# Gate/up weight sums of a tuned decoder trunk: two by DVE and two by accumulating DMA, and five whole pairs instead of six

## The chip, the core and the metric

The kernel runs on one core of a Trainium2 chip. The metric is the device time of one execution in microseconds, the median of several runs. Engines are called PE (TensorE matmul), PEld (its weight load), DVE (VectorE), ACT (ScalarE), POOL (GpSimd) and SP (SyncE, which here only issues DMAs).

## What is computed

A decoder trunk of two layers on 512 tokens of width 1024, all in float32. Each layer is half a SwiGLU feed-forward block, a mixer (MLA and GLA heads in layer 0, NSA in layer 1) and another half SwiGLU block; a final norm ends it. The change touches the four feed-forward blocks alone:

```python
def swiglu(x, w_gate, w_up, w_down):
    return (jax.nn.silu(x @ w_gate) * (x @ w_up)) @ w_down

for layer in range(DEPTH):           # DEPTH = 2, D_MODEL = 1024, D_FF = 2816, SEQ = 512
    h = h + 0.5 * swiglu(rms_norm(h, ffn_norm[layer, 0]), ...)
    ...                              # the mixer of this layer
    h = h + 0.5 * swiglu(rms_norm(h, ffn_norm[layer, 1]), ...)
```

## The kernel before

Activations lie as eight tiles of 128 channels x 512 tokens. Every float32 factor is split in two float32r parts, a high and a low one (`split`, L149: ACT casts to the high part at L150, DVE subtracts at L151 to get the low part), and every product is three matmuls (`mm3`, L143: L145 high x high, L146 with the low part of the activations, L147 with the low part of the weights).

A feed-forward block (`ffn_body`, L353) walks over 22 column blocks j of 128 hidden columns. A column block needs a gate weight g and an up weight u, each 128 x 1024 (eight chunks of 128 input channels side by side). There are two ways to do a block:

- **A whole pair** (`whole`, L367), for j below `NP` = 6: g and u are loaded, split, and multiplied with all eight chunks of the input, 2 x 8 x 3 matmuls of 512 columns. The result is scaled by `rb` (the norm's factor) afterwards, so whole pairs can start before the norm is known.
- **Seven products** (`gate_up` L117 for the weights, `gate_up_steps` L311 for the matmuls), for j from `NP` on. A Strassen-Winograd form of the 2 x 2 block product [g0 g1; u0 u1] x [x11 x12; x21 x22], where g0, g1 are the halves of g over input channels 0-511 and 512-1023, and the x parts are the input halves by channel and token: seven products of 4 x 3 matmuls of 256 columns. It wants four sums of weight halves (the two halves of tiles `sa` and `sb`, made by DVE at L130 to L133 from the raw loads of g and u) and seven forms of the input (`ffn_forms` L272, tiles `bh`/`bl`, which DVE makes at L283 to L300 and splits). The forms need `rb`, and four of the seven are split only when the last whole pair has let go of its input tiles (`xh`/`xl`), because they share 14 buffers.

The down projection is cut in units of 128 output channels (`unit`, L391): one load of 4 or 5 x 128 columns of w_down, its split, 12 or 15 matmuls into `ps_d`, and one DVE addition to the residual (L398). The units of one group of column blocks are spread over the blocks of the next.

All weight loads go by SP, in one queue, into three buffers `raw` of 512 KB; the split parts have three buffers `whi`/`wlo` (g and down weights) and three `shi`/`slo` (sums), and one `uhi`/`ulo`. The order on each engine is set by a scheduler from a modelled timeline; each engine then runs its list strictly in order and waits at semaphores. POOL does nothing in these stages.

## Time and profile before

| | before |
|---|---|
| median of 3 runs | 2013.54 us (2011.16 to 2014.27) |
| the profiled execution | 2011.51 us, of which the span of the core is 2009.7 us |
| PE, share of the span | 98% |
| DVE | 74% |
| ACT | 51% |
| POOL | 11% |
| mean granted TensorE clock | 0.994 |
| DMA traffic | 186.42 MB, mean 93 GB/s |

Busy shares are means over stages. The four feed-forward blocks lie at about 4 to 366, 596 to 950, 950 to 1304 and 1636 to 2008 us of the span; the mixers stand after the first and after the third. Time in the profile is counted from the first instruction; a matmul's row shows its way through the array, so rows overlap, and the pace is read from start to start.

### The profile page before, as it was taken

What the parts mean: (1) busy time and instruction counts of PE and PEld (TensorE: products, weight loads), DVE (VectorE), ACT (ScalarE), POOL (GpSimd) and SP (SyncE); (2) the same over time, 40 slices, a digit from 0 to 9 for tenths busy, and PEclk for the clock granted to TensorE, in tenths of its full rate; (3) what the DMA queues carried; (4) which work ended last, traced back from release to release, by engine and by line L of the source; (5) the groups of instructions that cost most, each with busy time, mean ns of one, the idle gap of its engine ahead of it and who ended that gap; (6) DMA issues with size and microseconds to landing.
All of it is one profiled execution on the core that took longest, in us unless ns stands there. A gap on an engine that the chain in (4) does not pass through costs nothing.

```text
span 2009.7 us, 31399 instructions
## 1 busy us (share of the span) xinstructions
PE 1969.0 (98%) x11986; PEld 1739.2 (87%) x11986; DVE 1491.5 (74%) x2557; ACT 1019.9 (51%) x1849; POOL 214.0 (11%) x255
## 2 busy tenths in 40 slices
PE   8999999999999999999999999999899999999998
PEld 6899998888778899998789999888687878999997
DVE  7877775678878777766877677667899868777774
ACT  6444443575764444444444444445598754444443
POOL 0000000201330000001000000111365410000001
PEclk9999999999999999999999999999899999999999
DMA  5333332321323233322323232344400033233332
GB/s 175 95 95 99 113 96 68 120 64 50 89 77 102 84 102 106 104 95 84 121 90 101 90 114 96 89 147 136 116 1 1 27 120 92 89 103 96 102 95 69
DMA packets 70553, 186.42 MB, mean 93 GB/s; under 512 B 9473, under 2 KB 12289, under 8 KB 70401
## 3 DMA queue, kind: packets, MB, share of 16 engines
q1 hardware_dynamic: 68944, 181.26, 29.2%
q10 hardware_dynamic: 1072, 2.10, 0.3%
q8 instruction: 94, 1.54, 0.3%
q0 software_dynamic: 384, 1.05, 0.2%
q14 instruction: 59, 0.48, 0.1%
HBM read 172.84 MB, written 2.10 MB: 87 GB/s over the span
## 4 chain that ended last, share of the span: by engine, by line
PE 88%; DVE 6%; ACT 2%; issue 2%; DMA 1%; POOL 0%; SPq 0%; ACTq 0%; POOLq 0%; DVEq 0%
PE ps_d L145 8%; PE ps_d L147 8%; PE ps_d L146 8%; PE ps_a L145 6%; PE ps_a L147 6%; PE ps_a L146 6%; PE ps_b L145 5%; PE ps_b L147 5%; PE ps_b L146 5%; PE ps_gu L147 4%; PE ps_gu L146 4%; PE ps_gu L145 4%; PE ps_p L145 3%; PE ps_p L146 3%; PE ps_p L147 3%
## 5 line engine op out<-in xcount | busy, mean ns | idle before, releaser
L150 ACT CAST whi<-raw 128x512 fp32r<-128x512 f32 (+3 forms) x317 | 257.7, 815 | 337.3 <-PE ps_d L146 124.7
L151 DVE TENSOR_TENSOR wlo<-raw,whi 128x512 fp32r<-128x512 f32 (+3 forms) x317 | 303.0, 957 | 80.6 <-ACT whi L150 79.1
L147 PE MATMUL ps_d<-hid,wlo 128*128 128x512 f32 x672 | 265.2, 396 | 0.0
L146 PE MATMUL ps_d<-hid,whi 128*128 128x512 f32 x672 | 264.9, 395 | 0.0
L145 PE MATMUL ps_d<-hid,whi 128*128 128x512 f32 x672 | 263.6, 395 | 0.0
L145 PE MATMUL ps_a<-bh,shi 128*128 128x256 f32 x768 | 216.9, 282 | 0.0
L146 PE MATMUL ps_a<-bl,shi 128*128 128x256 f32 x768 | 216.4, 282 | 0.0
L147 PE MATMUL ps_a<-bh,slo 128*128 128x256 f32 x768 | 216.2, 281 | 0.0
L216 POOL TENSOR_TENSOR ssq<-ssq,sq 128x512 f32<-128x512 f32 x30 | 46.1, 1538 | 1098.5 <-ACT sq L215 1098.5
L147 PEld LDWEIGHTS ps_d<-hid,wlo 128*128 128x128 f32 x672 | 126.1, 188 | 29.1 <-DVE wlo L151 0.7
L145 PEld LDWEIGHTS ps_d<-hid,whi 128*128 128x128 f32 x672 | 126.1, 188 | 27.1 <-ACT whi L150 1.0
L146 PEld LDWEIGHTS ps_d<-hid,whi 128*128 128x128 f32 x672 | 126.2, 188 | 25.2
L146 PEld LDWEIGHTS ps_a<-bl,shi 128*128 128x128 f32 x768 | 144.7, 188 | 1.2
L145 PEld LDWEIGHTS ps_a<-bh,shi 128*128 128x128 f32 x768 | 144.1, 188 | 1.2
L147 PEld LDWEIGHTS ps_a<-bh,slo 128*128 128x128 f32 x768 | 145.0, 189 | 0.0
L130 DVE TENSOR_TENSOR sa<-raw 128x512 f32<-128x512 f32 x64 | 44.2, 690 | 128.6 <-DMA raw<-wgu 128.6
L398 DVE SCALAR_TENSOR_TENSOR x<-ps_d,x 128x512 f32<-128x512 f32 x152 | 104.0, 686 | 44.3 <-PE ps_d L147 44.0
L612 POOL TENSOR_TENSOR pr<-pr,sums 128x128 f32<-128x128 f32 (+3 forms) x160 | 115.0, 748 | 101.1 <-DVE sums L1034 29.0
L150 ACT CAST uhi<-raw 128x512 fp32r<-128x512 f32 x64 | 39.7, 621 | 162.5 <-PE ps_b L146 104.0
L150 ACT CAST shi<-sa 128x1024 fp32r<-128x1024 f32 x64 | 67.3, 1051 | 80.1 <-PE ps_a L146 76.6
L151 DVE TENSOR_TENSOR slo<-sa,shi 128x1024 fp32r<-128x1024 f32 x64 | 78.3, 1223 | 29.3 <-ACT shi L150 27.3
L593 ACT ACTIVATE pr<-sm_s,sm_m 128x512 f32<-128x512 f32 (+3 forms) x160 | 89.7, 563 | 16.8 <-DVE sm_m L589 15.8
(452 smaller groups left out, 5583.2 us busy)
## 6 DMA issues: line engine op xcount, KB each, us to landing
raw<-wgu SPq DMA_DIRECT2D x175, 512.0 KB, 3.8
raw<-wd SPq DMA_DIRECT2D x96, 256.0 KB, 2.7
raw<-wd SPq DMA_DIRECT2D x64, 320.0 KB, 2.9
raw<-wo SPq DMA_DIRECT2D x32, 256.0 KB, 2.8
raw<-w1t SPq DMA_DIRECT2D x16, 512.0 KB, 3.8
raw<-w0v SPq DMA_DIRECT2D x8, 512.0 KB, 3.7
raw<-w0t SPq DMA_DIRECT2D x6, 512.0 KB, 3.7
rt_s<-rt_f SPq DMA_DIRECT2D x48, 64.0 KB, 2.0
```

What stands on the lines that cost most here:

```text
L130: V.tensor_add(av[:, :w], g[:, :w], u[:, :w])
L145: mm(ps, lh, rh, start=start, stop=False, **k)
L146: mm(ps, lh, rl, start=False, stop=False, **k)
L147: mm(ps, ll, rh, start=False, stop=stop, **k)
L150: self.nc.scalar.copy(hi, src)
L151: self.nc.vector.tensor_sub(lo, src, f32v(hi))
L216: (nc.vector if last or fast else nc.gpsimd).tensor_add(acc, acc, sq)
L398: V.scalar_tensor_tensor(out=self.x[c], in0=ps, scalar=0.5, in1=self.x[c], op0=ALU.mult, op1=ALU.add)
L593: nc.scalar.activation(p, s[:, :n], AF.Exp, bias=mn, scale=-1.0, accum_out=sums)
L612: self.nc.gpsimd.tensor_mul(o, o, w[:, qb : qb + 1].to_broadcast([P, n]))
```

## The change

- `NP` falls from 6 to 5: in each feed-forward block one column block goes from a whole pair to seven products (four in all; 68 blocks by seven products instead of 64). The generator that makes the input forms is run to its end before the first seven products, so that its six steps fit in five whole pairs.
- `gate_up` no longer loads u to a `raw` buffer. A new `load_sums`, traced two column blocks ahead, loads u to `sa` (512 KB) and the first half of u to `sb` (256 KB) by SP, behind the last weight load traced so far. Then two DMAs of 256 KB issued from POOL add in flight: g0 to `sb`'s first half, u1 to `sa`'s first half. DVE makes the other two sums (L141 and L142 of the changed kernel), the last of them into a new tile `sc`.
- `sa` and `sb` have two buffers each instead of one; the third pair of split parts (`uhi`/`ulo`) now holds `sc`. The sums are the same four up to sign and place, and the products take them in another order.

```diff
--- before.py
+++ after.py
@@ -27,7 +27,7 @@
 NEG = -1e30
 TINY = 1e-30
 GROUPS = ((0, 4), (4, 9), (9, 14), (14, 18), (18, 22))
-NP = 6
+NP = 5
 WARM = 11
 H = T // 2
 AHEAD = 400
@@ -88,7 +88,7 @@
         t = self.wp.tile([P, 1024], F32, name="raw", tag="raw", bufs=3)
         for i in range(parts):
             c = slice(i * n // parts, (i + 1) * n // parts)
-            self.nc.sync.dma_start(out=t[:, c], in_=src[:, c])
+            self.load = self.nc.sync.dma_start(out=t[:, c], in_=src[:, c])
         return t
 
     def wparts(self):
@@ -96,9 +96,6 @@
 
     def sparts(self):
         return (self.fw.tile([P, 1024], R, name=n, tag=n, bufs=3) for n in ("shi", "slo"))
-
-    def sum_tile(self, tag):
-        return self.fw.tile([P, 1024], F32, name=tag, tag=tag, bufs=1)
 
     def open_sums(self):
 
@@ -114,30 +111,41 @@
             self.split(raw[:, c], hi[:, c], lo[:, c])
         return hi, lo
 
+    def load_sums(self, f, j):
+
+        nc = self.nc
+        g, u = self.a["wgu"][f, j, 0], self.a["wgu"][f, j, 1]
+        h0, h1 = slice(0, T), slice(T, 2 * T)
+        av, bv = (self.fw.tile([P, 1024], F32, name=n, tag=n, bufs=2) for n in ("sa", "sb"))
+        with self.tc.issue_after(self.load.ins):
+            nc.sync.dma_start(out=bv[:, h0], in_=u[:, h0])
+            nc.sync.dma_start(out=av, in_=u)
+        nc.gpsimd.dma_start(out=bv[:, h0], in_=g[:, h0], accum_op=ALU.add)
+        nc.gpsimd.dma_start(out=av[:, h0], in_=u[:, h1], accum_op=ALU.add)
+        self.sums[j] = av, bv
+
     def gate_up(self, f, j):
 
 
         V, a = self.nc.vector, self.a
         w = T
+        h0, h1 = slice(0, w), slice(w, 2 * w)
+        av, bv = self.sums.pop(j)
+        cv = self.fw.tile([P, w], F32, name="sc", tag="sc", bufs=1)
         g = self.raw(a["wgu"][f, j, 0], 1024)
         gh, gl = self.wparts()
         self.split(g, gh, gl)
-        u = self.raw(a["wgu"][f, j, 1], 1024)
         ah, al = self.sparts()
         bh, bl = self.sparts()
-        uh, ul = (self.fw.tile([P, w], R, name=n, tag=n, bufs=1) for n in ("uhi", "ulo"))
-        av, bv = (self.sum_tile(n) for n in ("sa", "sb"))
-        V.tensor_add(av[:, :w], g[:, :w], u[:, :w])
-        V.tensor_add(av[:, w:], u[:, :w], u[:, w:])
-        V.tensor_add(bv[:, :w], av[:, w:], g[:, :w])
-        V.tensor_add(bv[:, w:], bv[:, :w], g[:, w:])
+        ch, cl = (self.fw.tile([P, w], R, name=n, tag=n, bufs=1) for n in ("uhi", "ulo"))
+        V.tensor_add(bv[:, h1], av[:, h0], g[:, h0])
+        V.tensor_add(cv, bv[:, h1], g[:, h1])
+        self.split(bv, bh, bl)
         self.split(av, ah, al)
-        self.split(bv, bh, bl)
-        self.split(u[:, w:], uh, ul)
-        h0, h1 = slice(0, w), slice(w, 2 * w)
+        self.split(cv, ch, cl)
         return [
-            (gh[:, h0], gl[:, h0]), (gh[:, h1], gl[:, h1]), (ah[:, h0], al[:, h0]), (bh[:, h0], bl[:, h0]),
-            (uh, ul), (ah[:, h1], al[:, h1]), (bh[:, h1], bl[:, h1]),
+            (gh[:, h0], gl[:, h0]), (gh[:, h1], gl[:, h1]), (bh[:, h0], bl[:, h0]), (bh[:, h1], bl[:, h1]),
+            (ah[:, h1], al[:, h1]), (ah[:, h0], al[:, h0]), (ch, cl),
         ]
 
     def mm3(self, ps, lh, ll, rh, rl, start, stop, **k):
@@ -358,6 +366,7 @@
         xs, end = self.ffn_input(gi)
         self.rb = None
         hid, todo, w, forms = {}, [], {}, []
+        self.sums = {}
 
         def done(j, gt, ut):
             V.tensor_mul(ut, gt, ut)
@@ -410,12 +419,16 @@
             g = next(i for i, (j0, j1) in enumerate(GROUPS) if j0 <= j < j1)
             if j == GROUPS[g][0] and g > 0:
                 todo += [(GROUPS[g - 1], c) for c in range(KC)]
+            if NP <= j + 2 < JC:
+                self.load_sums(f, j + 2)
             if NP <= j + 1 < JC:
                 w[j + 1] = self.gate_up(f, j + 1)
             if j < NP:
                 whole(j)
                 next(making, None)
                 if j == NP - 1:
+                    for _ in making:
+                        pass
                     cur = steps(NP)
                     next(cur)
             else:
```

The scheduler's order changes with it in the feed-forward blocks; in the mixers DVE and ACT keep theirs. Three places, all in the first block. A number in a name tells buffers and uses apart; `raw` is a weight load, `wgu` the gate/up and `wd` the down weights.

SP, in the middle of the seven-product blocks, before:

```order
L91 DMA raw_1581<-wd 128x640
L91 DMA raw_1604<-wd 128x640
L91 DMA raw_1627<-wgu 128x1024
L91 DMA raw_1633<-wgu 128x1024
L91 DMA raw_1756<-wd 128x640
L91 DMA raw_1779<-wd 128x640
L91 DMA raw_1802<-wgu 128x1024
L91 DMA raw_1808<-wgu 128x1024
```

and now:

```order
L91 DMA raw_1652<-wd 128x640
L121 DMA sb_1523<-wgu 128x512
L91 DMA raw_1675<-wd 128x640
L122 DMA sa_1522<-wgu 128x1024
L91 DMA raw_1705<-wgu 128x1024
L121 DMA sb_1699<-wgu 128x512
L91 DMA raw_1828<-wd 128x640
L91 DMA raw_1851<-wd 128x640
L122 DMA sa_1698<-wgu 128x1024
```

Between any two g loads there stood one u load and two down loads; now there stand a half and a whole u load for the sums, each in front of a weight load, with the accumulating DMAs on POOL's list.

DVE, blocks 8 to 10, before (L130 to L133 make the sums, L151 splits, L344 and L347 read products, L398 adds a down unit):

```order
L130 TENSOR_TENSOR sa_1291<-raw_1277,raw_1283 128x512
L131 TENSOR_TENSOR sa_1291<-raw_1283 128x512
L151 TENSOR_TENSOR hid_1105<-ut_908,hid_1105 128x512
L344 SCALAR_TENSOR_TENSOR ut_1077<-ps_b_1075,sx_1208 128x256
L151 TENSOR_TENSOR ulo_1141<-raw_1134,uhi_1140 128x512
L347 SCALAR_TENSOR_TENSOR ut_1077<-ps_a_1074,sw_1192 128x256
L151 TENSOR_TENSOR slo_1139<-sb_1143,shi_1138 128x1024
L398 SCALAR_TENSOR_TENSOR x_77<-ps_d_1263,x_77 128x512
L132 TENSOR_TENSOR sb_1292<-sa_1291,raw_1277 128x512
L133 TENSOR_TENSOR sb_1292<-sb_1292,raw_1277 128x512
```

and now (L159 splits, L352 and L355 read products, L407 adds a down unit, L141 makes a sum):

```order
L159 TENSOR_TENSOR slo_1060<-sa_876,shi_1059 128x1024
L407 SCALAR_TENSOR_TENSOR x_77<-ps_d_1182,x_77 128x512
L159 TENSOR_TENSOR wlo_1329<-raw_1326,whi_1328 128x512
L352 SCALAR_TENSOR_TENSOR ut_975<-ps_b_973,sx_1127 128x256
L355 SCALAR_TENSOR_TENSOR ut_975<-ps_a_972,sw_1111 128x256
L141 TENSOR_TENSOR sb_1197<-sa_1196,raw_1353 128x512
L159 TENSOR_TENSOR slo_1212<-sb_1047,shi_1211 128x1024
```

The first row frees the buffer into which `sa_1196` is loaded and accumulated; its reader stands five rows on, ahead of the split of the block before.

DVE where the last whole pair ends and the last four forms (`bl`) are split, before:

```order
L130 TENSOR_TENSOR sa_824<-raw_810,raw_816 128x512
L131 TENSOR_TENSOR sa_824<-raw_816 128x512
L151 TENSOR_TENSOR bl_739<-xf_269,bh_738 128x1024
L132 TENSOR_TENSOR sb_825<-sa_824,raw_810 128x512
L151 TENSOR_TENSOR slo_819<-sa_824,shi_818 128x1024
L133 TENSOR_TENSOR sb_825<-sb_825,raw_810 128x512
L151 TENSOR_TENSOR bl_743<-xf_267,bh_742 128x1024
L386 TENSOR_TENSOR gt_729<-ps_gu_673,rb_254 128x512
L151 TENSOR_TENSOR bl_747<-xf_266,bh_746 128x1024
L151 TENSOR_TENSOR wlo_793<-raw_790,whi_792 128x512
L151 TENSOR_TENSOR bl_751<-xf_268,bh_750 128x1024
L363 TENSOR_TENSOR ut_730<-gt_729,ut_730 128x512
```

and now:

```order
L159 TENSOR_TENSOR bl_635<-xf_269,bh_634 128x1024
L542 SCALAR_TENSOR_TENSOR rope_ang_519<-rope_k_520,rope_ang_519 128x512
L159 TENSOR_TENSOR bl_639<-xf_267,bh_638 128x1024
L542 SCALAR_TENSOR_TENSOR rope_ang_519<-rope_k_520,rope_ang_519 128x512
L159 TENSOR_TENSOR bl_643<-xf_266,bh_642 128x1024
L395 TENSOR_TENSOR ut_623<-ps_gu_597,rb_254 128x512
L159 TENSOR_TENSOR bl_647<-xf_268,bh_646 128x1024
L542 SCALAR_TENSOR_TENSOR rope_ang_519<-rope_k_520,rope_ang_519 128x512
L159 TENSOR_TENSOR slo_722<-sb_534,shi_721 128x1024
L407 SCALAR_TENSOR_TENSOR x_77<-ps_d_672,x_77 128x512
L372 TENSOR_TENSOR ut_623<-gt_622,ut_623 128x512
L159 TENSOR_TENSOR wlo_716<-raw_713,whi_715 128x1024
```

Before, four sums of the second seven-product block stood among the forms; now the split of that block's ready sum, `slo_722`, and the last of the rotary table's steps (`rope`) stand there.

## Rows read from the trace of the kernel before

**Rows 1.** The page: busy us of each engine, share of the span, instructions.
```profile
PE 1969.0 (98%) x11986; PEld 1739.2 (87%) x11986; DVE 1491.5 (74%) x2557; ACT 1019.9 (51%) x1849; POOL 214.0 (11%) x255
```

**Rows 2.** Groups by line and shape: busy us, mean ns | idle before.
```profile
L147 PE MATMUL ps_d<-hid,wlo 128*128 128x512 f32 x672 | 265.2, 396 | 0.0
...
L145 PE MATMUL ps_a<-bh,shi 128*128 128x256 f32 x768 | 216.9, 282 | 0.0
...
L145 PE MATMUL ps_gu<-xh,whi 128*128 128x512 f32 x192 | 76.4, 398 | 4.6 <-DVE gt L386 1.9 <-ACT whi L150 1.3 <-DVE x L580 0.9
```

**Rows 3.** PE's instructions in time, a whole pair: start us, duration us.
```profile
59.90 0.39 PE L145 MATMUL ps_gu<-xh,whi 128*128 128x512 f32 x1
...
69.70 0.39 PE L145 MATMUL ps_d<-hid,whi 128*128 128x512 f32 x1
```

**Rows 4.** The same, products of 256 columns.
```profile
200.03 0.28 PE L145 MATMUL ps_a<-bh,shi 128*128 128x256 f32 x1
...
205.43 0.28 PE L147 MATMUL ps_a<-bh,wlo 128*128 128x256 f32 x1
```

**Rows 5.** Busy time by stretch: first block's forms, other blocks' forms, seven-product stretch.
```profile
core 0: us, PE busy (x) PEld busy (x) DVE busy (x) ACT busy (x) POOL busy (x), PEclk, DMA share, GB/s
34.00:60.00 26.00, 24.09 (x104) 19.36 (x104) 25.78 (x42) 12.09 (x17) 0.00 (x0) 1.00 0.22 72
60.00:75.00 15.00, 15.00 (x66) 12.08 (x65) 14.33 (x22) 5.99 (x7) 0.00 (x0) 1.00 0.22 69
75.00:90.00 15.00, 15.00 (x71) 12.34 (x71) 11.44 (x16) 8.94 (x12) 0.00 (x0) 1.00 0.24 73
...
617.00:695.00 78.00, 78.00 (x390) 65.35 (x390) 62.92 (x92) 34.74 (x47) 0.00 (x0) 1.00 0.25 75
971.00:1049.00 78.00, 78.00 (x388) 65.13 (x387) 66.75 (x100) 36.45 (x50) 0.00 (x0) 1.00 0.26 78
1640.00:1718.00 78.00, 77.13 (x339) 62.21 (x340) 64.38 (x97) 39.39 (x49) 0.00 (x0) 1.00 0.31 97
...
730.00:900.00 170.00, 170.00 (x1157) 157.34 (x1156) 123.47 (x177) 74.85 (x124) 0.00 (x0) 1.00 0.32 100
```

**Rows 6.** Groups by line and shape: DVE's splits, sums and products of 512.
```profile
L151 DVE TENSOR_TENSOR wlo<-raw,whi 128x1024 fp32r<-128x1024 f32 x128 | 160.9, 1257 | 49.4 <-ACT whi L150 49.1
...
L363 DVE TENSOR_TENSOR ut<-gt,ut 128x512 f32<-128x512 f32 x88 | 60.2, 685 | 17.5 <-ACT gt L350 16.9
...
L130 DVE TENSOR_TENSOR sa<-raw 128x512 f32<-128x512 f32 x64 | 44.2, 690 | 128.6 <-DMA raw<-wgu 128.6
```

**Rows 7.** The page, DMA issues: KB each, median us from issue to landing.
```profile
raw<-wgu SPq DMA_DIRECT2D x175, 512.0 KB, 3.8
raw<-wd SPq DMA_DIRECT2D x96, 256.0 KB, 2.7
...
x<-xT SPq DMA_DIRECT2D x2, 512.0 KB, 7.6
...
kk<-ckv ACTq DMA_DIRECT2D x8, 128.0 KB, 3.5
...
kk<-ckv POOLq DMA_DIRECT2D x8, 127.8 KB, 3.5
```

**Rows 8.** POOL's instructions in time, around its DMAs.
```profile
1327.17 2.22 POOL L1135 DMA_DIRECT2D kk<-ckv  x4 [16.48 <-DVE ckv L1131]
```

**Rows 9.** DVE in time, a seven-product stretch: start us, duration us.
```profile
719.33 1.23 DVE L151 TENSOR_TENSOR slo<-sb,shi 128x1024 fp32r<-128x1024 f32 x1 [0.54 <-ACT shi L150]
...
722.12 0.82 DVE L151 TENSOR_TENSOR wlo<-raw,whi 128x640 fp32r<-128x640 f32 x1 [0.26 <-ACT whi L150]
```

**Rows 10.** PE in time: the first readers of those two.
```profile
723.08 0.28 PE L147 MATMUL ps_a<-bh,slo 128*128 128x256 f32 x1
...
726.43 0.39 PE L147 MATMUL ps_d<-hid,wlo 128*128 128x512 f32 x1
```

**Rows 11.** The waits of SP's queue, 34 to 340 us: us, times, longest.
```profile
SPq L91 <- DVE ulo L151: 55.9, 10, 9.7
```

## The prediction

> **What bounds the kernel now.** The page's busy shares come first: PE is busy 98% of the span, DVE 74%, POOL 11% [rows 1]. A busy PE can still wait, so the next view is the groups by line and shape, for the idle time ahead of a group: none ahead of the down products and of the seven products, 4.6 us in all ahead of the whole pairs [rows 2]. Third, PE's list in time: from the row at 59.90 to the row at 69.70 stand 42 steps, 0.2333 us each, with no gap [rows 3]; from 200.03 to 205.43 stand 45 steps of 0.1200 us [rows 4]. In the feed-forward blocks PE streams without a hole, at a granted clock of 1.00 (2.4 GHz) in every stretch listed [rows 5]. So only fewer matmul columns make these stages shorter; time saved on DVE, ACT or a queue is worth nothing by itself, and can only be lost if something comes late.
>
> **Fewer columns.** A whole pair is 2 x 8 x 3 = 48 matmuls of 0.2333 us, 11.20 us. Seven products are 7 x 4 x 3 = 84 of 0.1200 us, 10.08 us. One column block in each of four feed-forward blocks changes over: 4 x 1.12 = 4.48 us. All of it is on the path, and this is the only gain in the change.
>
> **Two sums fewer on DVE.** Four sums of about 0.69 us become two [rows 6], 1.4 us less per block and 95 us less in 68 blocks. In the seven-product stretch DVE is busy 123.5 of 170 us [rows 5], and PE does not wait for it. Value: 0. What it buys is cover for the next two terms.
>
> **The forms in a shorter time.** After the norm is known DVE makes and splits the input forms beside the whole pairs. In the first feed-forward block it is idle 0.22 us of 34 to 60, 0.67 of 60 to 75 and 3.56 of 75 to 90: 4.45 us in all [rows 5]. The change takes 11.20 us of PE's cover out of this stretch. With the pair go two splits of 1.26 and four operations of 0.69 (two products with the norm, the gate product, the hidden split) [rows 6]: 5.3 us. With two seven-product blocks prepared there, 2 x 1.4 us of sums go: 2.8. Missing are 11.2 - 5.3 - 2.8 = 3.1 us, and 4.45 are idle: it fits, by 1.3 us. In the other three blocks the stretches of 78 us hold 15.1, 11.3 and 13.6 us idle [rows 5], several times the 3.1. What is not idle when it is needed is the risk: the sum of block 6 wants its g load early, which SP issues behind 768 KB for the sums. I take 0.4 us lost, in the first block; the bounds are 0 and, if the spared sums help nothing in time (11.2 - 5.3 - 4.45 = 1.45 short) in every block, 5.8 us.
>
> **The accumulating DMAs.** No row shows one. Two are issued per block, 136 in all, of 256 KB each. On POOL an issue takes about 0.55 us (four in 2.22) [rows 8]; POOL has nothing else to do here and nobody queues behind it. To landing: a plain 256 KB load takes 2.7 us, 512 KB 3.8; the same 128 KB copy lands 3.5 us after its issue from POOL and from ACT, so POOL's queue is no slower; the slowest rows of this size, loads that started together with others, took 7.6 [rows 7]. An accumulate moves its own bytes and reads those of its destination, so I take the 512 KB row, 3.8 us, with 2.7 and 7.6 as bounds.
>
> Who waits: DVE, in order, at the first new sum. The tightest place is the second DVE pair above: the split of `sa_876` frees the buffer, `sa_1196` is loaded (3.8), POOL issues (0.55), the accumulate lands (3.8), 8.2 us in all, and five rows later DVE wants it. In between DVE also waits for PE anyway, for two products (L352, L355) that end about 6.4 and 7.8 us after the product whose weights' buffer let that split start (one product 1.44, a down unit 2.80, half a product 0.72, then 1.44 and 1.44). The split and its cast take 2.3 us of that time, so the data is there at 10.5, the sum could start at 8.2: DVE waits 2.3 us. A block lasts 10.08 + 24 x 0.2333 = 15.7 us on average; DVE was idle 27% of it, 4.3 us, and now has 1.4 more: 5.7 us. The wait lies inside. Behind it on DVE stand the split of the next block's sum and weight splits; before the change split parts were ready 2.5 us (at 720.56 for a reader at 723.08) and 3.5 us (722.94 for 726.43) ahead of PE [rows 9, 10]. Value: 0; at 2.7 us 0; at 7.6 us the wait is 6.1, 0.4 over the idle time.
>
> Against this speaks a rule of the Trainium skill (SBUF — State Buffer, section "SBUF: two separate sides"): descriptors of POOL's DMAs are written through a port pair that a DVE operation in a two-port mode holds to its end. By it an issue could come up to one long DVE operation later. No run here shows it, and the sum would stay 0 for this term, the wait 1.3 us longer.
>
> **More bytes in the queues.** SP issues per block 0.5 MB (g), 0.75 (sums) and 0.5 (down) for 1.5 before; with 0.5 accumulated that is 2.25, and 2.75 with what the accumulates read back. The DMA share of 0.32 [rows 5] grows to 0.48 or 0.59 in proportion. A down load behind a sum load lands 1.1 us later (256 KB) or 2.2 (512 KB), by the difference of the load rows [rows 7]; 2.5 to 3.5 us are spare. For it speaks that u no longer sits in a `raw` buffer: SP waited 55.9 us in ten waits for the last reader of u in the first feed-forward block [rows 11], and two or three loads per block now share three buffers where three or four did. Value: 0, upper bound with the second slower rival.
>
> **The sum.** -4.48 + 0.4 = -4.1 us. The profiled execution took 2011.51 us (span 2009.7, 1.8 around it), so it would take 2007.4; the median of before is 2.0 above that execution, and with the same distance the forecast is 2013.54 - 4.1 = **2009.4 us**, 0.21% less. A difference under 0.2% (4.0 us) can hardly be told from none here.
>
> **Rivals.**
> 1. *The forms eat the gain.* DVE is nearly saturated for 41 us of the first block [rows 5], and the shorter stretch makes PE wait at the first two seven-product blocks, 0.5 to 1.45 us in each feed-forward block. For it: the margin of 1.3 us is thin and in-order. Against: only the first block is that full. Loss 2 to 5.8: 2011 to 2015, middle about 2012. Chance 0.29.
> 2. *The accumulates come late* (slower). A price per block: the wait is 2.3 + (landing - 3.8); it decides from the point at which it passes 5.7, a landing of 7.2 us. At 7.6 us it is 0.4 us in each of 68 blocks, 27 us: 2036; each further 0.1 us costs 6.8. For it: no row shows the rate of an accumulate. Against: nothing but a doubled byte count is known to slow it. Chance 0.12.
> 3. *Weight loads land late behind the sums* (slower). It decides when down loads lose more than the spare 2.5 us; 0.1 to 0.3 us per block, 68 blocks, gives 7 to 20 us: 2016 to 2030. For it: a share of 0.59 and strict order in one queue. Against: the freed `raw` buffer. The Trainium skill (DMA: Bandwidth & Descriptors, section "Issuing engines are not separate DMA queues") adds that POOL's transfers run on the same 16 engines as SP's, so issuing the accumulates there separates nothing; the trace does not show it, and the 0.59 counts them together already. Chance 0.12.
> 4. *The whole gain, nothing lost:* 2009.1, part of the forecast's case.
>
> **How the numbers follow.** The forecast's case (loss 0 to 1.5 us, 2009.0 to 2010.6) has 0.47. It gives faster by over 0.2% only with a loss below 0.5 us, but the medians scatter by over 1 us either way: 0.38 of faster and 0.09 of the same; rival 1 gives 0.03 faster, 0.26 the same; rivals 2 and 3 are slower, 0.24. Faster 0.41, same 0.35, slower 0.24. The range takes in the scatter of the runs below the forecast (2009.1 - 2.1 = 2007.0), all of rival 1, and rival 3's lower end, to 2018; left out are rival 2 and the rest of rival 3, under 0.2.
>
> **What would show it.** Right: starts of 84 matmuls 0.1200 us apart where the sixth whole pair stood, no idle time ahead of `ps_a`, `ps_b` and `ps_d`, and DVE busy about 70% of the span. The forms' term: PE waits for a `bl` or `wlo` split within 60 us of the norm. The accumulates: their median landing, and DVE's wait ahead of L141, to be held against 2.3 us. The queue: the landing of `wd` loads against 2.7 and ACT's waits for them. Wrong: idle PE ahead of `ps_d` or `ps_a` in the middle of a feed-forward block, or a landing over 7 us.

## The result, and the profile after

| kernel | median us | ratio to before | 95% interval |
|---|---|---|---|
| before | 2012.7 | 1 | |
| after | 2027.9 (4 runs, 2025.2 to 2031.2) | 1.0076 | 1.0064 to 1.0088 |

The changed kernel is 15.2 us slower; 2009.4 was forecast, with 2018 as the upper end. The profiled execution has a span of 2026.4 us for 2009.7.

First the page of after: busy us, share of the span and instructions of each engine; then one group of instructions (busy us, mean ns | idle before), then DMA issues (KB each, median us to landing).

```profile
PE 1974.2 (97%) x12130; PEld 1750.6 (86%) x12130; DVE 1421.0 (70%) x2449; ACT 1031.1 (51%) x1873; POOL 333.3 (16%) x391
...
L123 POOL DMA_DIRECT2D sb<-wgu x68 | 59.4, 874 | 802.5 <-DMA sb<-wgu 353.8
...
sa<-wgu SPq DMA_DIRECT2D x68, 512.0 KB, 4.4
...
sb<-wgu POOLq DMA_DIRECT2D x68, 256.0 KB, 5.1
sa<-wgu POOLq DMA_DIRECT2D x68, 256.0 KB, 3.7
```

DVE fell from 74% to 70% [rows 1] as forecast, and bought nothing: the span grew by 17 us beside it. An accumulate takes POOL 0.87 us to issue (0.55 was taken from [rows 8]) and lands in 3.7 or 5.1 us (3.8 was taken from [rows 7]). None of this says where the time went.

PE's list does. These are the five matmuls of after's feed-forward blocks that waited longest because of the change (start us, duration us, and in brackets the idle time ahead and what ended it). Before the change, only the first of them waited, 1.9 us ([rows 2], the 1.9 behind `DVE gt`).

```profile
38.39 0.79 PE L153 MATMUL ps_gu<-xh,whi 128*128 128x512 f32 x1 [4.04 <-DVE gt L395]
...
624.08 0.51 PE L153 MATMUL ps_gu<-xh,whi 128*128 128x512 f32 x1 [0.99 <-DVE gt L395]
...
981.66 0.50 PE L153 MATMUL ps_gu<-xh,whi 128*128 128x512 f32 x1 [3.76 <-DVE gt L395]
...
1057.93 0.45 PE L153 MATMUL ps_a<-bh,uhi 128*128 128x256 f32 x1 [1.87 <-DVE ut L355]
...
1848.70 0.39 PE L153 MATMUL ps_b<-bh,shi 128*128 128x256 f32 x1 [2.54 <-DVE gt L342]
```

Three of the waits stand at the start of a block, at the third whole pair: its PSUM bank is free when DVE's product with the norm (L395) has read it. Two stand inside a block, at a product whose bank waits for an evacuation (L355, L342). All five end with DVE, which is idle 30% of the time.

The windows around four of them (us, busy us of each engine, granted clock, DMA share, GB/s) show a second loss:

```profile
core 0: us, PE busy (x) PEld busy (x) DVE busy (x) ACT busy (x) POOL busy (x), PEclk, DMA share, GB/s
36.00:46.00 10.00, 7.61 (x21) 6.04 (x22) 10.00 (x20) 5.61 (x8) 0.00 (x0) 0.66 0.19 47
1056.00:1062.00 6.00, 4.13 (x22) 4.07 (x22) 5.14 (x8) 1.34 (x3) 0.00 (x0) 0.72 0.14 32
981.00:988.00 7.00, 6.34 (x21) 5.03 (x22) 7.00 (x14) 4.38 (x6) 0.00 (x0) 0.76 0.10 36
1848.00:1855.00 7.00, 6.30 (x31) 5.59 (x32) 4.61 (x8) 3.21 (x7) 0.05 (x1) 0.76 0.30 95
```

The granted clock was 1.00 in every stretch of these blocks before [rows 5]. Now it falls to 0.5 (1.2 GHz) for some us around the end of each longer wait. Length times (1 - clock), summed over the four windows, is 3.4 + 1.7 + 1.7 + 1.7 = 8.5 us.

**Why L395 is late.** DVE at the start of the first block (start us, duration us):

```profile
31.46 0.88 DVE L192 TENSOR_SCALAR dg<-ident,rc 128x128 f32<-128x128 f32 x4
33.83 0.69 DVE L141 TENSOR_TENSOR sb<-sa,raw 128x512 f32<-128x512 f32 x1 [1.48 <-DMA sa<-wgu]
34.77 1.22 DVE L159 TENSOR_TENSOR wlo<-raw,whi 128x1024 fp32r<-128x1024 f32 x1 [0.26 <-ACT whi L158]
35.92 0.68 DVE L142 TENSOR_TENSOR sc<-sb,raw 128x512 f32<-128x512 f32 x1
36.52 1.22 DVE L159 TENSOR_TENSOR slo<-sb,shi 128x1024 fp32r<-128x1024 f32 x1
37.65 0.68 DVE L395 TENSOR_TENSOR gt<-ps_gu,rb 128x512 f32<-128x512 f32 x1
...
1051.46 0.42 DVE L352 SCALAR_TENSOR_TENSOR ut<-ps_b,sx 128x256 f32<-128x256 f32 x1 [0.99 <-PE ps_b L155]
1056.86 0.69 DVE L141 TENSOR_TENSOR sb<-sa,raw 128x512 f32<-128x512 f32 x1 [4.97 <-DMA sa<-wgu]
1057.47 0.41 DVE L355 SCALAR_TENSOR_TENSOR ut<-ps_a,sw 128x256 f32<-128x256 f32 x1
```

With five whole pairs the first unit of seven products is prepared one pair earlier, and its sums and splits now stand in DVE's list ahead of L395. DVE runs its list in order: it waits 1.48 us for the accumulate, does 3.8 us of work for a unit whose first product PE starts at 69.7, 32 us later, and only then frees the bank.

**Why L355 is late.** The last three of those rows are from inside the third block. L141 waits 4.97 us for the accumulate into `sa`, and the evacuation behind it waits with it. The chain in front of L141, on SP's queue and on POOL:

```profile
1046.37 0.33 SPq L122 DMA_DIRECT2D sa<-wgu  x1
...
1045.45 0.88 POOL L123 DMA_DIRECT2D sb<-wgu  x1 [9.74 <-ACT sx L348]
1053.16 0.86 POOL L124 DMA_DIRECT2D sa<-wgu  x1 [6.84 <-DMA sa<-wgu]
```

From the issue of the load to the sum it took 10.5 us. The load was slow, 6.1 us for a median of 4.4, and the DMA issues of 1040 to 1060 us show what ran beside it, the accumulate into `sb`. That this is what slowed it is not shown; e18 tries it.

```profile
sa<-wgu SPq DMA_DIRECT2D x1, 512.0 KB, 6.1
...
sb<-wgu POOLq DMA_DIRECT2D x1, 256.0 KB, 6.8
```

The Trainium skill (DMA: Bandwidth & Descriptors, section "Issuing engines are not separate DMA queues") says that transfers of all issuing engines run on the same DMA engines; these two rows, both slower than their medians, fit that.

### The profile page after: what moved, and what is told of

Its sections match the earlier page's. It is cut to its first block, busy times and chain, and to the rows that moved or that the text cites. A ratio compares the mean times of both kernels' runs of the same rounds, so it can differ in the third digit from the quotient of the medians.

```text
span 2026.4 us, 32299 instructions
## 1 busy us (share of the span) xinstructions
PE 1974.2 (97%) x12130; PEld 1750.6 (86%) x12130; DVE 1421.0 (70%) x2449; ACT 1031.1 (51%) x1873; POOL 333.3 (16%) x391
## 4 chain that ended last, share of the span: by engine, by line
PE 81%; DVE 8%; DMA 5%; issue 2%; ACT 2%; POOL 1%; SPq 0%; ACTq 0%; POOLq 0%; DVEq 0%
PE ps_d L153 7%; PE ps_d L154 7%; PE ps_d L155 7%; PE ps_a L153 6%; PE ps_a L155 6%; PE ps_a L154 6%; PE ps_b L153 5%; PE ps_b L155 4%; PE ps_b L154 4%; PE ps_p L153 3%; PE ps_p L154 3%; DMA sa<-wgu 3%; PE ps_p L155 3%; PE ps_gu L153 3%; PE ps_gu L154 3%; PE ps_gu L155 3%
## 5 line engine op out<-in xcount | busy, mean ns | idle before, releaser
L159 DVE TENSOR_TENSOR wlo<-raw,whi 128x512 fp32r<-128x512 f32 (+3 forms) x317 | 302.9, 962 | 59.6 <-ACT whi L158 58.9
L407 DVE SCALAR_TENSOR_TENSOR x<-ps_d,x 128x512 f32<-128x512 f32 x152 | 104.2, 687 | 116.5 <-PE ps_d L155 115.8
L158 ACT CAST shi<-sb 128x1024 fp32r<-128x1024 f32 x68 | 71.6, 1053 | 194.5 <-PE ps_a L154 190.0
L153 PE MATMUL ps_b<-bh,shi 128*128 128x256 f32 x544 | 154.4, 284 | 3.0 <-DVE gt L342 2.9
L153 PE MATMUL ps_a<-bh,shi 128*128 128x256 f32 x544 | 153.8, 283 | 0.0
L155 PE MATMUL ps_b<-bh,slo 128*128 128x256 f32 x544 | 153.5, 282 | 0.0
L154 PE MATMUL ps_b<-bl,shi 128*128 128x256 f32 x544 | 153.5, 282 | 0.0
L154 PE MATMUL ps_a<-bl,shi 128*128 128x256 f32 x544 | 153.2, 282 | 0.0
L155 PE MATMUL ps_a<-bh,slo 128*128 128x256 f32 x544 | 153.0, 281 | 0.0
L153 PEld LDWEIGHTS ps_b<-bh,shi 128*128 128x128 f32 x544 | 102.2, 188 | 6.7 <-DVE gt L342 4.0
L154 PEld LDWEIGHTS ps_b<-bl,shi 128*128 128x128 f32 x544 | 102.8, 189 | 2.5
L155 PEld LDWEIGHTS ps_b<-bh,slo 128*128 128x128 f32 x544 | 103.2, 190 | 0.0
```

What stands on the lines that cost most here:

```text
L153: mm(ps, lh, rh, start=start, stop=False, **k)
L154: mm(ps, lh, rl, start=False, stop=False, **k)
L155: mm(ps, ll, rh, start=False, stop=stop, **k)
L158: self.nc.scalar.copy(hi, src)
L159: self.nc.vector.tensor_sub(lo, src, f32v(hi))
L407: V.scalar_tensor_tensor(out=self.x[c], in0=ps, scalar=0.5, in1=self.x[c], op0=ALU.mult, op1=ALU.add)
```

## The experiments

Theory A, from this reading: the time is lost where a sum that waits for its accumulate stands in DVE's list ahead of an evacuation that PE waits for, and in the half clock behind each such wait. Theory B: making the input forms beside fewer pairs costs it (rival 1). Theory C: the bytes make weight loads late (rival 3).

The table holds all runs, and for the profiled execution of each the length of the four feed-forward blocks. Each is cut at the first product of the first unit: *start* runs from the first matmul of the first whole pair to there, *inside* from there to the start of the last down matmul, both in us from PE's list. Outside the four blocks, where no run changes anything, these profiled executions also differ, from 581.8 us (e17) to 589.7 (e16), so they are compared block by block.

| kernel | median us | ratio, 95% interval | block 1 start / inside | block 2 | block 3 | block 4 |
|---|---|---|---|---|---|---|
| before (six pairs) | 2012.7 | 1 | 74.7 / 284.1 | 74.7 / 279.0 | 75.2 / 279.0 | 76.0 / 282.8 |
| after | 2027.9 | 1.0076 (1.0064 to 1.0088) | 63.2 / 300.1 | 54.6 / 299.4 | 59.6 / 303.0 | 54.1 / 309.0 |
| e1 | 2021.8 | 1.0040 (1.0027 to 1.0053) | 62.6 / 299.8 | 55.0 / 299.8 | 55.9 / 299.8 | 54.1 / 303.6 |
| e2 | 2013.2 | 1.0001 (0.9992 to 1.0010) | 61.1 / 299.8 | 53.4 / 299.1 | 55.1 / 299.1 | 54.1 / 304.1 |
| e3 (six pairs) | 2025.1 | 1.0074 (1.0050 to 1.0098) | 81.0 / 280.4 | 74.6 / 280.3 | 75.8 / 281.2 | 76.1 / 284.6 |
| e5 | 2015.8 | 1.0019 (1.0010 to 1.0028) | 58.2 / 299.8 | 52.8 / 301.2 | 55.2 / 299.8 | 54.0 / 306.3 |
| e9 | 2033.3 | 1.0109 (1.0092 to 1.0126) | 65.7 / 296.7 | 58.7 / 296.9 | 65.2 / 298.2 | 59.2 / 300.0 |
| e11 | 2011.8 | 0.9984 (0.9971 to 0.9997) | 61.5 / 299.8 | 52.8 / 299.8 | 53.0 / 299.8 | 54.1 / 303.6 |
| e12 | 2019.7 | 1.0034 (1.0021 to 1.0047) | 59.8 / 299.8 | 52.8 / 299.8 | 55.9 / 299.8 | 54.1 / 310.1 |
| e13 | 2011.5 | 0.9993 (0.9983 to 1.0003) | 58.1 / 299.9 | 52.8 / 299.8 | 53.3 / 299.8 | 54.1 / 304.1 |
| e14 (six pairs) | 2023.9 | 1.0055 (1.0041 to 1.0069) | 75.0 / 284.1 | 74.7 / 279.0 | 75.1 / 280.4 | 76.0 / 293.0 |
| e15 | 2010.0 | 0.9985 (0.9976 to 0.9994) | 58.7 / 299.8 | 52.8 / 299.8 | 54.6 / 299.8 | 54.8 / 303.4 |
| e16 (four pairs) | 2016.7 | 1.0019 (1.0010 to 1.0028) | 48.8 / 313.1 | 41.5 / 311.3 | 42.7 / 312.8 | 42.9 / 314.9 |
| e17 = e11 | 2009.9 | 0.9982 (0.9972 to 0.9991) | 58.5 / 299.8 | 52.7 / 299.8 | 53.0 / 299.8 | 54.1 / 303.6 |
| e18 | 2024.4 | 1.0054 (1.0037 to 1.0071) | 61.1 / 305.3 | 52.7 / 301.2 | 54.1 / 304.9 | 54.1 / 304.6 |

Five pairs without a loss read 58.5 / 299.8, 52.7 / 299.8, 53.0 / 299.8 and 54.1 / 303.6 (e17). Against that, after loses 4.7 + 1.9 + 6.6 + 0.0 = 13.2 us at the starts and 0.3 - 0.4 + 3.2 + 5.4 = 8.5 inside.

**e1: five pairs alone.** The kernel before with

```diff
-NP = 6
+NP = 5
...
                 if j == NP - 1:
+                    for _ in making:
+                        pass
                     cur = steps(NP)
```

> The kernel before with five whole pairs for six and nothing else: all four sums stay on VectorE and no transfer is added. Theory A (the changed kernel loses its time where a late accumulate holds VectorE's list, and in the half clock behind each stall): the column gain shows, 4 x 1.12 us, less 0 to 2 us because the first block's sums stand ahead of the norm's evacuation: 2008 to 2011 us. Theory B (making the input forms beside fewer whole pairs is what costs): most of the loss is here too, 2015 to 2028. Theory C (more bytes in the queues make weight loads late): no bytes are added, 2008 to 2010.

2021.8 us: not what theory A said, and in theory B's range. Without any accumulate the kernel is slower than before. The table, from an execution of 2016.9 us, shows where: inside the blocks nothing is lost, at the starts 4.1 + 2.3 + 2.9 us against e17. DVE (first fence) and PE (second) at the first start:

```profile
32.83 0.68 DVE L132 TENSOR_TENSOR sb<-sa,raw 128x512 f32<-128x512 f32 x1
33.43 0.17 DVE L201 RECIPROCAL rc<-rs_q 128x4 f32<-128x4 f32 x1
33.54 0.69 DVE L133 TENSOR_TENSOR sb<-sb,raw 128x512 f32<-128x512 f32 x1
...
35.60 1.22 DVE L151 TENSOR_TENSOR slo<-sa,shi 128x1024 fp32r<-128x1024 f32 x1
37.58 0.69 DVE L386 TENSOR_TENSOR gt<-ps_gu,rb 128x512 f32<-128x512 f32 x1 [0.77 <-ACT rb L167]
```
```profile
35.83 1.10 PE L186 MATMUL ps_b<-dg,ones 128*128 128x512 f32 x2 [2.52 <-DVE dg L184]
38.33 0.79 PE L145 MATMUL ps_gu<-xh,whi 128*128 128x512 f32 x1 [1.40 <-DVE gt L386]
```

The four sums stand between the small rows of the norm, and PE waits first for the norm and then for the bank. So a late accumulate is not needed for the loss at the start; the place in the list is. Theory A had named the place, but put at most 2 us on it and the rest on late accumulates: there it was wrong. From here on it stands for any work for a later unit ahead of such an evacuation.

**e2: after without the accumulates.** After, with

```diff
-        nc.gpsimd.dma_start(out=bv[:, h0], in_=g[:, h0], accum_op=ALU.add)
-        nc.gpsimd.dma_start(out=av[:, h0], in_=u[:, h1], accum_op=ALU.add)
```

> The changed kernel without its two accumulating transfers per unit; the plain loads of both buffers, their bytes and their place in SP's queue stay. Two of four sums are left out, so the output is another. Theory A: no sum waits for an accumulate, the stalls at about 38, 624, 982, 1058, 1768 and 1849 us and the half clock behind them go: 2007 to 2011 us, granted clock 0.994 as before. Theory B: 2018 to 2028, the forms are unchanged. Theory C: 1.25 of the 1.75 MB that the change handles for g and its sums are left in the queue, so a good part stays: 2014 to 2024.

2013.2 us, 2 above the range for theory A; nothing is lost inside, and of the starts 2.6 us in the first block and 2.1 in the third, where the two sums that are left still stand ahead of the norm's product. Theory C's range begins at 2014, and e13 below decides.

**e5: the order at the start.** After, with

```diff
+        with ExitStack() as st:
+            if j == NP:
+                st.enter_context(self.tc.issue_after(self.evac2.ins))
-        V.tensor_add(bv[:, h1], av[:, h0], g[:, h0])
-        V.tensor_add(cv, bv[:, h1], g[:, h1])
+            V.tensor_add(bv[:, h1], av[:, h0], g[:, h0])
+            V.tensor_add(cv, bv[:, h1], g[:, h1])
```

where `evac2` is the product with the norm of the second pair.

> The changed kernel with one order forced: in each feed-forward block, the first unit's two sums on VectorE stand behind the evacuation of the first two whole pairs (the product with the norm) instead of ahead of it. Theory A: the stalls at the starts of the blocks and their half clock go (2.1 + 3.4 us in the first, 1.1 in the second, 3.9 + 1.7 in the third), 12 us less: 2014 to 2019 us; the stalls at 1058, 1768 and 1849 stay. Theories B and C: it moves no form and no byte: 2025 to 2031.

2015.8 us, 12 less than after, as theory A said. DVE, and PE's wait at the same place:

```profile
34.23 1.23 DVE L162 TENSOR_TENSOR wlo<-raw,whi 128x1024 fp32r<-128x1024 f32 x1 [1.97 <-ACT whi L161]
35.37 0.68 DVE L398 TENSOR_TENSOR gt<-ps_gu,rb 128x512 f32<-128x512 f32 x1
...
37.76 0.68 DVE L144 TENSOR_TENSOR sb<-sa,raw 128x512 f32<-128x512 f32 x1
```
```profile
36.11 0.49 PE L156 MATMUL ps_gu<-xh,whi 128*128 128x512 f32 x1 [1.71 <-DVE gt L398]
```

The product with the norm starts at 35.4 for 37.7, the wait is that of before, and the clock stays 1.00 there. What is left against e17 is 2.2 us at the start of the third block and 1.4 + 2.7 inside the second and fourth.

**e9: the order inside.** After, with the sums and splits of each unit traced behind the seventh product of the unit ahead, and the first sum queued behind its evacuation (L355, kept as `evac`):

```diff
+        def rest(late=None):
+            with ExitStack() as st:
+                if late:
+                    st.enter_context(self.tc.issue_after(late.ins))
+                V.tensor_add(bv[:, h1], av[:, h0], g[:, h0])
...
                 next(cur, None)
                 cur = nxt
+                if j + 1 < JC:
+                    self.rest(self.evac)
```

> The changed kernel with the other order forced: from the second unit on, the first sum stands on VectorE behind the evacuation for which the seventh product of the unit ahead waits, so a late accumulate no longer holds that one up. Theory A: the stalls at 1058, 1768 and 1849 and the half clock behind them go (2.0 + 1.7, 0.5, 2.7 + 1.7), 8.6 us less, if the later sums are still in time for the third product: 2017 to 2022 us; the stalls at the starts stay. Theory C: unchanged, 2025 to 2031. A further case: the sums now come too late, and a new wait of PE shows ahead of the third product of each unit: over 2030.

2033.3 us, a miss. The waits at L355 and L342 are gone from PE's list, but a new one came up at the end of all four blocks (three of them in this group: busy us, mean ns | idle before):

```profile
L159 PE MATMUL ps_d<-hid,whi 128*128 128x512 f32 x672 | 264.8, 396 | 5.5 <-ACT hid L164 5.5
```

To trace the sums later also moved PE's list: in after a down unit of an earlier group follows the last product (350.76), in e9 none is left, and PE waits for the last column block's way into `hid`, from 350.9 to 352.75 in the first block. The edit changed more than it meant to, so it confirms the place and not the price.

**e11, e17: five pairs, VectorE's sums, the order at the start.** e1, with

```diff
+        with ExitStack() as st:
+            if j == NP:
+                st.enter_context(self.tc.issue_after(self.evac2.ins))
```

around its four sums. e17 is the same kernel in more rounds.

> The kernel before with five whole pairs for six, all four sums on VectorE, and the first unit's sums forced behind the evacuation of the first two pairs. In the run with five pairs alone PE stood 2.7 + 1.6, 2.1 and 0.8 + 1.8 us at the starts of three feed-forward blocks. Theory A (the order at the block's start is what five pairs cost, not the forms): those stalls fall to those of before, and the whole column gain of 4.5 us is left: 2007 to 2010 us. Theory B (the forms do not fit beside fewer pairs): stalls of the same size come back a few us later, 2012 or more.

> The same kernel as in the run with five pairs, VectorE's sums and the forced order at the start, in more rounds, for a narrower interval: five of its executions took 2005 to 2007 us and five or six 2011 to 2013. Columns alone say 2008. If the order at the start is all that five pairs cost, the median lies at 2007 to 2011 us, below the kernel before by 0.1 to 0.3%.

2011.8 and 2009.9 us, 0.9984 and 0.9982: faster than before, by an interval that excludes 1. (The second expectation miscounts: four of e11's ten executions took 2005.0 to 2007.3 us, six 2011.7 to 2013.1.) One order turns e1's 0.40% loss into a 0.18% gain. The blocks of e17 are shorter than those of before by 0.5, 1.2, 1.4 and 1.1 us, 4.2 in all, beside 4 x 1.12 of columns. Theory B is out for five pairs.

**e16: four pairs.** e11, with

```diff
-NP = 5
+NP = 4
```

> The kernel before with four whole pairs for six, all sums on VectorE, the first unit's sums forced behind the norm's evacuation. Theory A: another 4.5 us of columns go if the forms still fit beside four pairs in all four blocks: 2003 to 2008 us. Theory B: one more pair's cover, 11.2 us, is too much; TensorE waits ahead of the first seven products: 2012 to 2030.

2016.7 us: theory B holds one pair further. PE now waits in the first units, where DVE is still at the forms:

```profile
76.50 0.50 PE L149 MATMUL ps_d<-hid,whi 128*128 128x512 f32 x1 [0.77 <-DVE hid L154]
80.64 0.38 PE L148 MATMUL ps_b<-bh,uhi 128*128 128x256 f32 x1 [1.42 <-DVE gt L337]
```

**e13: e5 without the accumulates.** The edit of e2, made in e5.

> The changed kernel with the first unit's sums behind the norm's evacuation, and without the two accumulating transfers per unit (two of four sums left out, so the output is another); the plain loads for the sums stay. Theory A: what is left of the loss in the run with that order alone (2015.8) is late accumulates inside the blocks (787, 1758, 1837 us) and the clock behind them, so it goes: 2007 to 2010 us. Theory C (bytes of the plain loads): 2012 to 2016.

2011.5 us, between the two ranges, and no loss inside the blocks but 0.5 us. The plain loads for the sums, 0.75 MB per unit, cost at most the difference to e17, 0.11% with intervals that overlap. So theory C is out for these loads; the bytes of the accumulates are left to e15 and e18.

**e3: six pairs with the accumulates.** After, with the line below; the first sum then stands behind the product with the norm by itself.

```diff
-NP = 5
+NP = 6
```

> The changed kernel with six whole pairs again: accumulates and their loads alone, no column less. The first sum of each block stands behind the norm's evacuation here. Theory A: no stalls at the starts, some late accumulates inside the blocks (1 to 3 us each with the clock, 64 units for 68): 2013 to 2020 us. Theory C: 0.1 to 0.3 us in each unit: 2018 to 2030. If accumulates cost nothing by themselves: 2011 to 2013.

2025.1 us, above the range for theory A and inside theory C's. The accumulates cost 12 us alone. The four blocks are 2.6, 1.2, 2.8 and 1.9 us longer than before (the cut between start and inside lies elsewhere in this order); PE waits in six units, 0.2 to 1.1 us each, ahead of `ps_b`, and each of these waits ends with DVE's evacuation L342, none with a weight split, as theory C would have it. Its four runs spread from 2020.8 to 2030.7, and the profiled one is the shortest, with no half clock inside the blocks; what the longer ones lost beyond it is in no trace.

**e12: the sum of u loaded earlier.** e5 with a third buffer for `sa` in the first three blocks (`ahead` is 3 there, 2 in the last, which has no room):

```diff
             if NP <= j + 2 < JC:
-                self.load_sums(f, j + 2)
+                self.load_sums(f, j + 2, "sb")
+            if NP <= j + self.ahead < JC:
+                self.load_sums(f, j + self.ahead, "sa")
```

> The changed kernel with the first unit's sums behind the norm's evacuation and, in the first three feed-forward blocks, a third buffer for the sum of u and its load and accumulate traced three units ahead for two (the last block has no room for it). Theory A: the wait inside the second block (787 us, 1.3 us and its clock) goes, those in the last block (1758, 1837) stay: 2012 to 2015 us. If an earlier load only crowds out weight loads (theory C): 2016 or more.

2019.7 us, a miss, in the range for theory C. Inside the three blocks with the third buffer nothing is lost any more (299.8 each), as expected. The loss comes mainly from the last block, 310.1 for 306.3: its units still run two ahead, and one wait of 2.5 us ahead of `ps_a`, ended by DVE's evacuation and with half clock behind it, hit another unit than in e5. Why that unit was hit this time is not shown.

**e15: the accumulate into sa made by DVE.** e5 without the second accumulate, and

```diff
+            V.tensor_add(av[:, h0], av[:, h0], av[:, h1])
             V.tensor_add(bv[:, h1], av[:, h0], g[:, h0])
```

with the order at the start for the first two units.

> The changed kernel with the first units' sums behind the norm's evacuation, and the accumulate into sa, for which VectorE's first sum waits, made by VectorE from the two halves of the loaded u; the accumulate into sb stays. Theory A (the chain load, accumulate, first sum is what is late): it is 5 us shorter now, the stalls inside the blocks go: 2009 to 2013 us against 2015.8 with both. Theory C (the accumulates' bytes slow the weight loads): half of the accumulated bytes stay, and half of the loss: 2013 to 2015.

2010.0 us, 0.9985: the loss inside is gone, not half of it as theory C had it, and one accumulate per unit is free. DVE's waits for `sa` in after and in e15 (us in total, times, longest):

```profile
DVE sb L141 <- DMA sa<-wgu: 51.8, 20, 5.3
```
```profile
DVE sa L143 <- DMA sa<-wgu: 74.1, 42, 4.9
```

DVE waits longer for `sa` in e15 than in after, and inside the blocks PE no longer waits, though evacuations stand straight behind such waits here too. One place (DVE, and PE at the product that needs the bank of L358):

```profile
1086.22 0.69 DVE L143 TENSOR_TENSOR sa<-sa 128x512 f32<-128x512 f32 x1 [4.87 <-DMA sa<-wgu]
1086.83 0.42 DVE L355 SCALAR_TENSOR_TENSOR ut<-ps_b,sx 128x256 f32<-128x256 f32 x1
1087.16 0.41 DVE L358 SCALAR_TENSOR_TENSOR ut<-ps_a,sw 128x256 f32<-128x256 f32 x1
```
```profile
1088.82 0.28 PE L156 MATMUL ps_a<-bh,uhi 128*128 128x256 f32 x1
```

Most of the 4.87 us passed before there was anything to evacuate: the product that L358 reads ended at 1085.1, so L358 started 2.1 us behind it, and it was done 1.2 us before PE needed the bank. In after's third block L355 started 4.6 us behind its product. Neither the sum of an engine's waits nor the row behind a wait gives the price; how late the wait ends does, against the product that is read and the one that needs the bank.

**e18: only the accumulate into sa.** e5 without load and accumulate of `sb`, and

```diff
             V.tensor_add(bv[:, h1], av[:, h0], g[:, h0])
+            V.tensor_sub(bv[:, h0], bv[:, h1], av[:, h1])
```

> The changed kernel with the first unit's sums behind the norm's evacuation and only the accumulate into sa kept; the sum in sb is made by VectorE (one subtraction from the next sum), and its load and accumulate are gone. Theory A1 (the chain sa load, accumulate, first sum is too long by itself): the stalls inside the blocks stay, 2013 to 2017 us, as with both accumulates (2015.8). Theory A2 (the chain is late only where the accumulate into sb runs beside the load of sa and stretches it, 6 to 7 us for 4.4): the load of sa falls to some 4 us everywhere and the stalls go, 2008 to 2011 us, as with the accumulate into sb alone (2010.0).

2024.4 us, worse than with both, beyond A1's range and far from A2's. The median load of `sa` fell only to 4.0 us, and the chain is still late in some units:

```profile
1159.81 0.81 DVE L161 TENSOR_TENSOR wlo<-raw,whi 128x640 fp32r<-128x640 f32 x1
1166.09 0.69 DVE L142 TENSOR_TENSOR sb<-sa,raw 128x512 f32<-128x512 f32 x1 [5.47 <-DMA sa<-wgu]
1166.70 0.42 DVE L344 TENSOR_TENSOR gt<-ps_b,sa 128x256 f32<-128x256 f32 x1
```
```profile
1167.17 0.39 PE L155 MATMUL ps_b<-bh,shi 128*128 128x256 f32 x1 [2.84 <-DVE gt L344]
```

So the two steps in a row are the cause, with `sb`'s accumulate beside them or not: without them (e15) the loss is gone, with them alone it stays. Why it is more than with both was not tried; DVE has one operation more per unit here than in after, but so it has in e15.

**e14: a delay of known size.** The kernel before, with the evacuation of its L347 repeated in column block 12:

```diff
-            V.scalar_tensor_tensor(out=ut[:, H:], in0=z, ...
+            for _ in range(1 + again):
+                V.scalar_tensor_tensor(out=ut[:, H:], in0=z, ...
```

> The kernel before with one delay in each feed-forward block, in the unit of column block 12: the evacuation for which the seventh product waits is repeated 6, 9, 15 and 24 times more on VectorE (the same value each time, 0.34 us apart). No transfer and no pair is changed. With 1.0 us of slack and up to 2 us of other rows between them TensorE should stand about 1 to 3, 2 to 4, 4 to 6 and 7 to 9 us. Theory A (a stall in the middle of a block is followed by a half clock): behind those of 2 us and more the granted clock is 0.5 for 3.4 to 6.8 us, which costs another 1.7 to 3.4 us each; 2030 to 2045 us in all. If the clock does not follow a stall: the granted clock stays 1.00 there and the time grows by the stalls alone, 14 to 22 us, 2026 to 2035.

2023.9 us, below both ranges, since the first two delays were hidden whole and the third nearly so: there was more to spare than the expectation's 1.0 us. The two that PE felt, and the clock around them:

```profile
1148.30 0.39 PE L145 MATMUL ps_a<-bh,shi 128*128 128x256 f32 x1 [1.11 <-DVE ut L348]
...
1848.93 0.58 PE L145 MATMUL ps_a<-bh,shi 128*128 128x256 f32 x1 [7.63 <-DVE ut L348]
```
```profile
1148.00:1160.00 12.00, 11.70 (x96) 11.66 (x97) 11.12 (x18) 7.21 (x15) 0.00 (x0) 1.00 0.22 58
1842.00:1856.00 14.00, 7.07 (x39) 7.08 (x40) 10.59 (x21) 3.67 (x8) 0.00 (x0) 0.63 0.00 0
```

The first left the clock at 1.00 and made its block longer by 1.4 us. The second took it to 0.5 for 14 x (1 - 0.63) / 0.5 = 10.4 us, from 1844 on, so about half of that while PE still stood, and the block grew by 10.2 us: 7.6 of wait and 2.6 of clock. This long wait cost more than its length.

## Why the prediction was wrong, step by step

**Fewer columns: right.** 4.48 us forecast; e17's blocks give back 4.2. By the medians it is 3.3 us in e17 and 0.9 in e11, the same kernel, by the ratios of all their runs 3.6 and 3.2.

**Two sums fewer: right at 0.** e15 (three sums on DVE) and e17 (four) take the same time, 0.9985 and 0.9982.

**The forms in a shorter time: right by its sum, wrong in what it asked.** It weighed DVE's work against DVE's idle time from 34 to 90 us and found room for 1.3 us. There is room: in e11 and e17 the loss is gone, and e16 shows the limit one pair further. (Its bound of 5.8 us takes the first block's shortfall four times, though the rows give the other blocks several times the idle time; and rival 1's loss of 2 to 5.8 us has its middle near 2013, not 2012.) But the step asked how much DVE has to do in the stretch, not in which order. With one pair less the first unit's preparation moves ahead of the product with the norm, for which PE's third pair waits. That is the failed step: 0.4 us (at most 5.8) was forecast, and the order at the start is worth 2027.9 - 2015.8 = 12 us in after and 2021.8 - 2009.9 = 12 in e1. In DVE's order of the two kernels it could be read ahead: the first sum stands four rows ahead of L395 after the change.

**The accumulating DMAs: right chain, wrong cover.** Forecast were 3.8 + 0.55 + 3.8 = 8.2 us from load to sum; by the medians it is 4.4 + 3.7 = 8.1, the issue's 0.87 within the second. DVE's wait was to be 2.3 us in every unit; it is 51.8 us in 20 places. Both are near enough or better. What failed is "the wait lies inside": 5.7 us of idle time, an average over a block, were held against it. Idle time elsewhere in the block does not help a row that stands behind the waiting one, and behind L141 stand, in some units, L355 or L342, and not only the splits. In the trace before, 1.4 to 4.5 us lie between the end of the first of these evacuations (there L347) and the product that needs its bank, 2.0 to 4.5 for the other (there L334). So a wait of the size forecast was mostly covered: in after, 2.72 us ahead of L355 (1748.60) and 2.69 ahead of L342 (1089.31) cost PE nothing; 3.11 (1766.24) cost it 0.36, 4.97 (1056.86) 1.87 and 5.32 (1845.35) 2.54. One typical wait stood in the sum for all 68 units, and the few long ones cost the time: 8.5 us inside the blocks in the profiled execution, and 0.34% or 6.8 us by e5 against e15. Rival 2 named this mechanism, and set its point of decision at a median landing of 7.2 us. The median stayed at 3.7; the slow units decided, such as the one with 6.8 us from load to issue and 3.7 to landing.

The rule weighed at this step, that POOL's descriptors wait for a two-port operation of DVE (the Trainium skill, SBUF — State Buffer, section "SBUF: two separate sides"), does not show in the issue times: of the 136 issues of accumulates in after, the 44 beside a DVE busy for under 20% of the issue have a median of 0.87 us, the 41 beside one busy for over 80% of it 0.87 as well, the longest 1.01. The trace does not tell whether any of these DVE operations was in a two-port mode, so the rule itself is neither shown nor refuted.

**More bytes in the queues: right at nearly 0** (e13 against e17). The DMA share over 730 to 900 us is 0.52 in after, for 0.32 before and 0.48 to 0.59 forecast.

**A step that was not there: the clock.** The sum let a wait cost its length. In after the five waits shown are 4.04 + 0.99 + 3.76 + 1.87 + 2.54 - 1.91 (before's own) = 11.3 us, and the half clock adds up to 8.5: with 4.2 of columns given back, 15.6 of the 17.5 us by which the four blocks grew. e14 shows the clock's part without any of the change's edits.

**The balance.** -4.5 (columns) + 12 (order at the start, its clock within) + 6.8 (accumulate into `sa`, its clock within) = 14.3 us, beside 15.2 measured. This checks the size alone: the price of the accumulates is not one number, 6.8 us here and 12 at six pairs (e3), and which units run late differs from run to run of the table.

## What to carry to other kernels

Before a share of idle time is used as cover, find the row of the in-order engine at which the new wait stands, and price what stands behind it: a wait ahead of a PSUM evacuation comes out of TensorE as soon as it ends later than that evacuation can spare, however idle the engine is elsewhere. Price the longest waits, not the typical one. When a stage is shortened, read the new order around its hand-over: work for a later stage that moves ahead of the evacuation costs as much as a late transfer, and one forced order gives it back. Of several transfers in a row, keep the one off the DMA queues whose result is read first (e15).

## What was not expected of the hardware

The granted clock after a wait of PE in the middle of a stream: 1.1 us (e14, 1148) left it at 1.00; 1.87 us (after, 1057.9) and 2.54 (1848.7) took it to 0.5 for 3.4 us, 4.04 at 38.4 for 6.8, and 7.63 (e14) for about 10 (a window's length times one minus its clock, over 0.5). It was not the same each time: a wait of 1.95 us at 624.4 in e1 left no mark, nor did one of 2.43 at 37.8 in e12. e11 and e17 are one kernel, and PE waits 1.40 us at the same matmul of the first start in both (behind 1.14 and 0.62 us ahead of the norm's matmul); over 34 to 46 us the granted clock was 0.86 in e11 and 1.00 in e17. With 0.83 over 8 to 18 us and 0.79 over 548 to 556, both 1.00 in e17, that is 5.1 of the 8.0 us between their profiled executions. So the clock's share of a loss read from one trace is in part luck. The Trainium skill (TensorE: Matmul & The Clock Gate, section "Why this matters for your kernels") warns that idle gaps between bursts take the engine back to its lower clock; these rows agree in that, but here gaps shorter than the page's limit did it, and the measurement decides.

Two accumulates of the same 256 KB land in 5.1 and 3.7 us: the slower is the one into `sb`, which runs beside the 512 KB load of `sa` in 64 of 68 units. With `sb`'s gone (e18), the one into `sa` still takes 3.8.
